# Hybrid mixer layer: two more pairs of input tiles in seven products, retention's output written over its queries, and the right operands started after the first retention

## The chip, the cores and the metric

The kernel runs on one core of one Trainium2 chip. The metric is device microseconds of one execution; a comparison uses the median of several runs. A profile is one execution recorded by the hardware profiler.

## The reference

One decoder layer over 1024 positions of width 1024, in float32. Cut to what matters here:

```python
u = rms_norm(x, norm1_g)
z = u @ w_in                                    # 3584 columns, 28 tiles of 128
cb, cc, ch = split(z[..., :1536], 3)            # conv group, 512 channels
rq, rk, rv, rg = split(z[..., 1536:], 4)        # retention group, 4 heads of 128
y_conv = group_rms_norm(cb * causal_dwconv3(cc * ch, conv_w), conv_norm_g, 8)
q, k = rotary(rq), rotary(rk) * 128 ** -0.5
o = chunkwise_retention(q, k, rv)               # chunks of 128, decay per head
y_ret = group_rms_norm(o, ret_norm_g, 4) * silu(rg)
x = x + concat([y_conv, y_ret]) @ w_out
x = x + relu(rms_norm(x, norm2_g) @ w_up) ** 2 @ w_down
out = rms_norm(x, final_norm_g)
```

Retention works chunk by chunk: `(q k^T * decay) v` inside a chunk, plus `q` times a state carried from chunk to chunk.

## The kernel before

Activations lie transposed: features on the 128 partitions, positions along the row, so a tile `u` has 128 features and 1024 positions in two halves of 512. Each float32 factor is split into a high and a low part of a faster matmul type (`uh`, `ul` for the activations, `wh`, `wl` for a weight piece of 512 input features by 128 outputs), and a product takes three matmuls, high by high, low by high, high by low. ACT casts a raw weight piece `r` to `wh`, and DVE or POOL subtracts to get `wl` (`split_piece`). Four pieces are prepared ahead; each of the pools behind `r`, `wh` and `wl` has four buffers.

The mixer goes through these stages on PE:

- The values `v` (line 343), then eight tiles for queries and keys of two head pairs (`rot_tiles`, four tiles for each pair).
- `retention(p, q, k)` for a pair of heads, a generator in ten steps (eight chunks and two to drain). A step puts small 128x128 matmuls on PE: scores and transposed keys of chunk c, output and new state of chunk c-1, transposed output of chunk c-2. It also puts work on DVE and ACT. The first one runs while the second pair's queries and keys are multiplied, the second while the next tiles are.
- The eight tiles 0 to 7 of `IN_WHOLE`, one after the other, each by `tile_in` in 48 matmuls of 128x512 (four quarters of 12). Tiles 3i, 3i+1, 3i+2 are the three columns of conv group i. Their evacuation (`whole`, `use`) reads the PSUM bank at once.
- The four pairs of tiles of `IN_PAIRS`, each by `pair_in`: a Strassen scheme (two by two blocks in seven products instead of eight) of 7 x 12 matmuls. The left operands are sums of weight blocks, built on POOL (`Left`), and split on the fly. The right operands are the blocks `11`, `21`, `22` of `u` and four sums `t1` to `t4`, which `rights(j)` makes from freshly loaded `x` rows (`xs`) for j = 0 to 3: two DMAs, two scalings on ACT, four subtractions and three splits on DVE or POOL. `t1` is written over the second halves of `uh[0..3]`, `ul[0..3]` when the whole tiles are done. After each product DVE adds the bank to the partial sums `z`.
- When all mixer work is done, the output projection begins (operands `yh`, `yl`). Its PSUM pools take the place of the mixer's, so its first matmul waits for the last read of a mixer bank.

The order on each engine is written by a planner at build time. Engines are objects with a modelled clock; `now[0]` is the modelled PE time. After each slot of PE work (`slot`, `SLOT`), `tick` runs `background`, which lets the waiting tasks (retention, rights, conv, gate, norm) issue instructions: a task that yields `None` runs once its `ready` time lies `PE_MARGIN` back, one that yields a number once it lies that number back, one that yields engines when one of them is free within `look`, one that yields a key when `mark` has set it. `force(key)` runs everything until the key is set. Each engine then executes its queue strictly in the order written. All input DMAs are on SP's queue.

Columns of the last pair go in the order `IN_LAST = (1, 2, 6, 7, 4, 5, 3)`, which keeps two partial sums by ACT copies of the running sum `acc`.

Of the kernel before, what the change touches and what calls it, by code (L numbers as in the profile page):

```python
# [23 lines left out]
NC_ = T // P  # L24
# [10 lines left out]

IN_WHOLE = [[0, 1, 2], [3, 4, 5, 6, 7]]
IN_PAIRS = [(8, 9), (10, 11), (20, 21), (22, 23)]
IN_FIRST = [12, 13, 16, 17, 14, 15, 18, 19] + IN_WHOLE[0] + IN_WHOLE[1]  # L40
SLOT, LOOK, PE_MARGIN, LATE = 2.72, 2.0, 1.2, 0.0
NORM_MARGIN = 4.0
UP_ORDER, MLP_ORDER = (1, 2, 5, 6, 3, 7, 4), (1, 2, 6, 5, 3, 7, 4)
IN_LAST = (1, 2, 6, 7, 4, 5, 3)

# [33 lines left out]
def hybrid_layer(  # L79
# [16 lines left out]
    now, clock, procs, got = [0.0], {}, [], {}  # L96
# [23 lines left out]
    def unit(dt=F32, s="u"):  # L120
        return big.tile([P, T], dt, tag="u", name=nm(s))
# [439 lines left out]
    def retention(p, q, k):  # L561

        h0 = 2 * p
        S = pend = turn = None
        o = [unit(s="o") for _ in range(2)]
        js = [slice(j * P, (j + 1) * P) for j in range(2)]
        if p:
            yield "retention", 0
        for c in range(NC_ + 2):
            yield None  # L570
            now[0] += 2.0
            new = None
            if c < NC_:
                sl = slice(c * P, (c + 1) * P)
                bs = bank(pr)
                for j in range(2):
                    nc.tensor.matmul(bs[:, js[j]], k[j][:, sl], q[j][:, sl], start=True, stop=True)  # L577
                kz = None
                if c < NC_ - 1:
                    bt = bs[:, 2 * P :]  # L580
                    for j in range(2):
                        nc.tensor.transpose(bt[:, js[j]], k[j][:, sl], ident)
                sc = xp.tile([P, 2 * P], F32, tag="h", name=nm("h"), bufs=6)
                for j in range(2):
                    dve.scalar_tensor_tensor(
                        sc[:, js[j]], bs[:, js[j]], by_key[:, h0 + j, c : c + 1], causal,
                        ALU.mult, ALU.mult,
                    )
                if c < NC_ - 1:
                    kz = xp.tile([P, 2 * P], F32, tag="h", name=nm("h"), bufs=6)  # L590
                    for j in range(2):
                        act.activation(
                            kz[:, js[j]], bt[:, js[j]], AF.Copy, scale=by_state[:, h0 + j, c : c + 1]
                        )
                new = (c, sc, kz)
            done, pend = pend, new
            turned, turn = turn, None
            if done is not None:
                pc, sc, kz = done
                psl = slice(pc * P, (pc + 1) * P)  # L600
                vt = v[pc // 2]
                v0 = (pc % 2) * H + h0 * P
                vj = [vt[:, v0 + j * P : v0 + (j + 1) * P] for j in range(2)]
                bo = bank(pr)
                for j in range(2):
                    nc.tensor.matmul(bo[:, js[j]], sc[:, js[j]], vj[j], start=True, stop=(S is None))  # L606
                    if S is not None:
                        nc.tensor.matmul(  # L608
                            bo[:, js[j]], q[j][:, psl], S[:, js[j]], start=False, stop=True
                        )  # L610
                if kz is not None:
                    bk = bo[:, 2 * P :]
                    for j in range(2):
                        nc.tensor.matmul(bk[:, js[j]], kz[:, js[j]], vj[j], start=True, stop=True)  # L614
                    Sn = xp.tile([P, 2 * P], F32, tag="S", name=nm("S"), bufs=2)
                    if S is None:
                        dve.tensor_copy(Sn, bk)
                    else:
                        for j in range(2):
                            dve.scalar_tensor_tensor(  # L620
                                Sn[:, js[j]], S[:, js[j]], gammas[h0 + j] ** P, bk[:, js[j]],
                                ALU.mult, ALU.add,
                            )
                    S = Sn

                on = xp.tile([P, 2 * P], F32, tag="h", name=nm("h"), bufs=6)
                m = xp.tile([P, 2], F32, tag="m", name=nm("m"), bufs=4)
                for j in range(2):
                    act.activation(
                        on[:, js[j]], bo[:, js[j]], AF.Square, accum_out=m[:, j : j + 1]  # L630
                    )
                dve.scalar_tensor_tensor(
                    m, m, 1.0 / P, by_query[:, h0 : h0 + 2, pc], ALU.mult, ALU.add
                )
                m = rsqrt(m, xp.tile([P, 2, 2], F32, tag="m2", name=nm("m"), bufs=4))
                for j in range(2):
                    act.activation(on[:, js[j]], bo[:, js[j]], AF.Copy, scale=m[:, j : j + 1])
                turn = (pc, on)
            if turned is not None:
                pc, on = turned  # L640
                b = bank(pr)
                for j in range(2):
                    nc.tensor.transpose(b[:, js[j]], on[:, js[j]], ident)
                for j in range(2):
                    act.copy(o[j][:, pc * P : (pc + 1) * P], b[:, js[j]])
                    if pc % 4 == 3:
                        o_n[h0 + j, pc // 4] = o[j]
                        mark(("o", h0 + j, pc // 4), act)
            retention_task[p].ready = max(clock[act], clock[dve])
            if c == NC_:  # L650
                mark(("retention", p), act)

# [111 lines left out]

    def rights(j):

        if j:
            yield "retention", 1
        a, b = xs[j], xs[4 + j] = [unit(s="xs") for _ in range(2)]
        lo_, hi_ = hs  # L770
        for k, t in ((j, a), (4 + j, b)):
# [42 lines left out]
    def pair_in(fs, last):  # L814
# [3 lines left out]
        for at, n in enumerate(order):  # L818
# [9 lines left out]
            if n == 2:  # L828
                dve.tensor_add(c11, acc, b)
                ready = 0, 0  # L830
            if n in (6, 7, 4):
                dve.tensor_add(acc, acc, b)
            if n == 4:
                ready = 1, 0
            if last:

                if n == 6:
                    act.copy(c12, acc)
                if n == 7:
                    act.copy(c22, acc)  # L840
                if n == 5:
                    dve.tensor_add(c22, c22, b)
                    dve.tensor_add(c12, c12, b)
                    ready = 1, 1
            else:
                if n == 5:
                    b5 = b
                if n == 6:
                    dve.tensor_add(c12, acc, b5)
                if n == 7:  # L850
                    dve.tensor_add(c22, acc, b5)
                    ready = 1, 1
# [477 lines left out]
    last = None  # L1330
# [147 lines left out]
```

## Time and profile before

| | |
|---|---|
| three runs | 1091.83, 1095.05, 1096.20 us; median 1095.05 |
| profiled execution | 1093.19 us, of which the span shown is 1091.4 us |
| busy over the span | PE 97%, DVE 80%, POOL 51%, ACT 43% |
| values and first 8 tiles | up to about 158 us |
| whole tiles 0 to 7 | about 158 to 266 us |
| four pairs | 266.4 to 350.9 us on PE |
| first matmul of the output projection | 362.75 us |

The rest of the span, from 362.75 us on, is the output projection and the MLP, which the change does not touch. In the views, PE, DVE, ACT, POOL and SP are the engines; a row of the time line has start, duration, engine, line, operation, output<-input, count, and in square brackets the idle time before it and what ended it. Nearly all DVE, ACT and POOL work is issued by one helper on line 73, so it is told apart by the tile names.

### The profile page before, as it was taken

What the parts mean: (1) busy time and instruction counts of PE and PEld (TensorE: products, weight loads), DVE (VectorE), ACT (ScalarE), POOL (GpSimd) and SP (SyncE); (2) the same over time, 40 slices, a digit from 0 to 9 for tenths busy, and PEclk for the clock granted to TensorE, in tenths of its full rate; (3) what the DMA queues carried; (4) which work ended last, traced back from release to release, by engine and by line L of the source; (5) the groups of instructions that cost most, each with busy time, mean ns of one, the idle gap of its engine ahead of it and who ended that gap; (6) DMA issues with size and microseconds to landing.
All of it is one profiled execution on the core that took longest, in us unless ns stands there. A gap on an engine that the chain in (4) does not pass through costs nothing.

```text
span 1091.4 us, 13980 instructions
## 1 busy us (share of the span) xinstructions
PE 1056.6 (97%) x4916; PEld 882.4 (81%) x4916; DVE 870.2 (80%) x1239; ACT 468.3 (43%) x920; POOL 558.1 (51%) x385
## 2 busy tenths in 40 slices
PE   7999999999898799989999999999999999999996
PEld 6888888887786588878888888888888888888886
DVE  7436655569988756599999989989899899899945
ACT  8211346556345444444333443443344344334453
POOL 5234343227667313448639448267276285384543
PEclk9999999999999899999999999999999999999998
DMA  7121121140111535050121211211201301210204
GB/s 271 61 59 38 40 78 40 29 155 11 58 58 45 197 97 183 1 174 20 49 87 30 69 58 40 79 37 52 91 24 49 97 20 49 88 29 11 78 1 155
DMA packets 38870, 76.50 MB, mean 70 GB/s; under 512 B 4368, under 2 KB 6544, under 8 KB 38800
## 3 DMA queue, kind: packets, MB, share of 16 engines
q1 hardware_dynamic: 38800, 75.61, 21.5%
q8 instruction: 39, 0.64, 0.3%
q14 instruction: 31, 0.25, 0.1%
HBM read 68.78 MB, written 6.82 MB: 69 GB/s over the span
## 4 chain that ended last, share of the span: by engine, by line
PE 84%; DVE 7%; issue 4%; ACT 2%; POOL 2%; DMA 1%; SPq 0%; DVEq 0%; POOLq 0%; ACTq 0%
PE b L387 56%; PE b L1228 22%; PE b L343 2%; DVE wl L73 2%; DVE x L73 1%; DVE z L73 1%; ACT wh L73 1%; PE b L606 1%; PE b L577 1%; DVE t L73 1%; POOL r L73 1%; PE b L608 1%; PE b L614 1%; PE b L324 1%; DMA wv<-w_v 1%
## 5 line engine op out<-in xcount | busy, mean ns | idle before, releaser
L73 ACT CAST wh<-r 128x512 fp32r<-128x512 f32 x286 | 177.0, 621 | 347.4 <-PE b L387 169.7
L73 DVE TENSOR_TENSOR wl<-r,wh 128x512 fp32r<-128x512 f32 x256 | 238.1, 932 | 95.7 <-ACT wh L73 93.7
L387 PE MATMUL b<-U,wh 128*128 128x512 f32 x992 | 306.0, 389 | 3.3 <-DVE U L73 3.0
L73 POOL TENSOR_TENSOR r<-r,r 128x512 f32<-128x512 f32 x136 | 210.2, 1548 | 122.4 <-DVE wl L73 70.7
L1228 PE MATMUL b<-V,wh 128*128 128x512 f32 x784 | 241.9, 389 | 0.4 <-POOL V L73 0.4
L387 PEld LDWEIGHTS b<-U,wh 128*128 128x128 f32 x992 | 186.0, 188 | 42.7 <-DVE U L73 3.4
L73 DVE TENSOR_TENSOR x<-x,b 128x512 f32<-128x512 f32 (+1 forms) x320 | 197.9, 664 | 25.0 <-PE b L387 22.1
L387 PE MATMUL b<-U,wl 128*128 128x512 f32 x496 | 193.0, 389 | 0.0
L1228 PEld LDWEIGHTS b<-V,wh 128*128 128x128 f32 x784 | 147.2, 188 | 31.8 <-POOL V L73 0.8
L73 POOL TENSOR_TENSOR t<-t,t 128x512 f32<-128x512 f32 x70 | 105.5, 1511 | 99.2 <-ACT t L73 53.2
L1228 PE MATMUL b<-V,wl 128*128 128x512 f32 x392 | 152.5, 389 | 0.0
L73 POOL TENSOR_TENSOR wl<-r,wh 128x512 fp32r<-128x512 f32 x30 | 40.8, 1360 | 148.2 <-ACT wh L73 142.1
L387 PE MATMUL b<-ul,wh 128*128 128x512 f32 x320 | 104.9, 393 | 4.5 <-DVE ul L73 4.5
L387 PEld LDWEIGHTS b<-U,wl 128*128 128x128 f32 x496 | 93.1, 188 | 19.4
L387 PE MATMUL b<-uh,wh 128*128 128x512 f32 x320 | 106.3, 397 | 0.0
L387 PE MATMUL b<-uh,wl 128*128 128x512 f32 x320 | 104.3, 391 | 0.0
L1228 PEld LDWEIGHTS b<-V,wl 128*128 128x128 f32 x392 | 73.6, 188 | 15.1
L73 POOL TENSOR_TENSOR V<-t,V 128x512 fp32r<-128x512 f32 x35 | 49.1, 1402 | 67.2 <-ACT V L73 67.2
L73 DVE TENSOR_TENSOR t<-t,b 128x512 f32<-128x512 f32 x112 | 75.8, 677 | 1.7 <-POOL t L73 1.2
L387 PEld LDWEIGHTS b<-ul,wh 128*128 128x128 f32 x320 | 60.4, 189 | 17.8 <-DVE ul L73 4.9
L73 ACT ACTIVATE t<-t 128x512 f32<-128x512 f32 x64 | 40.2, 631 | 76.8 <-DVE t L73 76.1
L387 PEld LDWEIGHTS b<-uh,wl 128*128 128x128 f32 x320 | 60.5, 189 | 13.0
(164 smaller groups left out, 1456.4 us busy)
## 6 DMA issues: line engine op xcount, KB each, us to landing
r<-w_up_t SPq DMA_DIRECT2D x64, 256.0 KB, 2.6
r<-w_down_t SPq DMA_DIRECT2D x56, 256.0 KB, 2.6
r<-w_in_t SPq DMA_DIRECT2D x48, 256.0 KB, 2.6
xt<-xT SPq DMA_DIRECT2D x16, 256.0 KB, 5.4
xs<-xT SPq DMA_DIRECT2D x8, 512.0 KB, 5.4
r<-w_out_t SPq DMA_DIRECT2D x16, 256.0 KB, 2.6
x<-xT SPq DMA_DIRECT2D x8, 512.0 KB, 7.3
outT<-out SPq DMA_DIRECT2D x6, 512.0 KB, 2.9
```

The source lines that it names most:

```text
L73: return f(out, *args, **kw)
L324: nc.tensor.matmul(b[:, c * P : (c + 1) * P], d, ident, start=True, stop=True)
L343: nc.tensor.matmul(vb[i], a[k][:, tsl], b[k // 2][:, vs], start=(k == 0 and a is uh and b is vh), stop=(k == KT - 1 and a is ul),)
L387: nc.tensor.matmul(b, a[:, k, :], rhs(n, k)[r], start=(start and i == 0), stop=(stop and i == len(ops) - 1),)
L577: nc.tensor.matmul(bs[:, js[j]], k[j][:, sl], q[j][:, sl], start=True, stop=True)
L606: nc.tensor.matmul(bo[:, js[j]], sc[:, js[j]], vj[j], start=True, stop=(S is None))
L608: nc.tensor.matmul(bo[:, js[j]], q[j][:, psl], S[:, js[j]], start=False, stop=True)
L614: nc.tensor.matmul(bk[:, js[j]], kz[:, js[j]], vj[j], start=True, stop=True)
L1228: nc.tensor.matmul(b, a, r, start=(i == 0), stop=(i == len(ops) - 1))
```

## The change

Tiles 4 to 7 leave the whole tiles and become the pairs (4,5) and (6,7), ahead of the four pairs there were. The retention writes its output chunk into the query tile it has just used (`o = q`) instead of two new tiles. `rights(0)` and `rights(1)` start after the first retention (1 when 0 is done), 2 and 3 after the second, where 1 to 3 waited for the second before. A retention step may follow 0.3 instead of 1.2 behind its `ready` time, which is now the DVE time of its scores or state, not the later of ACT and DVE at its end; the planner looks 3.2 instead of 2.0 ahead. In the last pair two DVE additions take the place of two ACT copies.

```diff
-IN_WHOLE = [[0, 1, 2], [3, 4, 5, 6, 7]]
-IN_PAIRS = [(8, 9), (10, 11), (20, 21), (22, 23)]
+IN_WHOLE = [[0, 1, 2], [3]]
+IN_PAIRS = [(4, 5), (6, 7), (8, 9), (10, 11), (20, 21), (22, 23)]
...
-SLOT, LOOK, PE_MARGIN, LATE = 2.72, 2.0, 1.2, 0.0
-NORM_MARGIN = 4.0
+SLOT, LOOK, PE_MARGIN, LATE = 2.72, 3.2, 1.2, 0.0
+NORM_MARGIN, STEP_MARGIN = 4.0, 0.3
...
-        o = [unit(s="o") for _ in range(2)]
+        o = q
...
-            yield None
-            now[0] += 2.0
+            yield STEP_MARGIN
+            now[0] += 1.7
...
                 new = (c, sc, kz)
+                retention_task[p].ready = clock[dve]
...
                     S = Sn
+                    retention_task[p].ready = clock[dve]
...
-            retention_task[p].ready = max(clock[act], clock[dve])
+            if c >= NC_ - 1:
+                retention_task[p].ready = clock[act]
...
-        if j:
-            yield "retention", 1
+        yield "retention", j // 2
+        if j == 1:
+            yield "t4", 0
...
+            if last and n in (6, 7):
+                dve.tensor_add(c12 if n == 6 else c22, acc, b)
             if n in (6, 7, 4):
                 dve.tensor_add(acc, acc, b)
...
-                if n == 6:
-                    act.copy(c12, acc)
-                if n == 7:
-                    act.copy(c22, acc)
```

In all, 24 matmuls of 128x512 go (four tiles of 48 become two pairs of 84). DVE gets 26 instructions more, ACT 4 and POOL 4; SP issues as many DMAs as before.

The first place is DVE's queue where the second retention ends and the late right operands begin. `m` are the retention's small norm factors, `xs` and `U` the right operands, `z<-b,R` the evacuation of a whole tile. Before, this stands behind tile 4 (`a_1940` and `cv_2124` are conv group 1):

```order
L73 TENSOR_TENSOR m_2098<-m_2098 128x2
L73 SCALAR_TENSOR_TENSOR m_2098<-m_2098,m_2094 128x2
L73 SCALAR_TENSOR_TENSOR m_2098<-m_2098 128x2
L73 TENSOR_TENSOR a_1940<-a_1940,ssq 128x512
L73 SCALAR_TENSOR_TENSOR cv_2124<-a_1940,sm,cv_2124 128x511
L73 SCALAR_TENSOR_TENSOR cv_2124<-a_1940,sm,cv_2124 128x510
L73 SCALAR_TENSOR_TENSOR cv_2124<-a_1940,sm,cv_2124 128x512 x2
L73 TENSOR_TENSOR xs_2110<-xs_2110 128x512
L73 TENSOR_TENSOR xs_2110<-xs_2111,xs_2110 128x512
```

Now it stands around the evacuation of tile 2 (`z_1968`):

```order
L73 TENSOR_TENSOR m_1926<-m_1926 128x2
L73 SCALAR_TENSOR_TENSOR m_1926<-m_1926,m_1922 128x2
L73 SCALAR_TENSOR_TENSOR m_1926<-m_1926 128x2
L73 TENSOR_TENSOR U_1946<-xs_1613,U_1946 128x512
L73 TENSOR_TENSOR z_1968<-b_1790,R 128x512
L73 TENSOR_TENSOR z_1968<-b_1791,R 128x512
L73 TENSOR_TENSOR z_1968<-z_1968,cv_1786 128x512 x2
L73 TENSOR_TENSOR xs_1938<-xs_1938 128x512
L73 TENSOR_TENSOR xs_1938<-xs_1939,xs_1938 128x512
```

The last step of the second retention has moved from behind tile 4 to the end of tile 2, the right operands of j = 0 and 1 (`U_1946` is the last of them) are done by then, and those of j = 2 (`xs_1938`) follow tile 2. From this first `xs` row to the last addition of the last pair DVE's queue held 119 instructions before and holds 152 now.

The second place is ACT's queue in the last pair. `wh` are the casts of weight pieces, `yh` those of finished outputs. Before:

```order
L73 CAST wh_3008<-r_2771 128x512
L73 COPY z_2939<-z_2940 128x512
L73 ACTIVATE z_2939<-z_2939 128x512
L73 CAST yh_3019<-z_2588 128x512
L73 CAST wh_3038<-r_2894 128x512
L73 COPY z_2940<-z_2940 128x512
L73 CAST yh_3044<-o_834 128x512
L73 CAST yh_3048<-o_835 128x512
L73 CAST wh_3068<-r_2930 128x512
```

and now:

```order
L73 ACTIVATE z_2966<-z_2966 128x512
L73 CAST wh_3040<-r_2801 128x512
L73 CAST yh_3048<-q_604 128x512
L73 CAST yh_3051<-q_605 128x512
L73 CAST wh_3070<-r_2938 128x512
L73 CAST wh_3094<-r_2959 128x512
L73 CAST yh_3099<-q_943 128x512
L73 CAST wh_3121<-r_2985 128x512
```

The two `COPY z` rows, each of which reads a sum that DVE must have written, no longer stand ahead of the weight casts.

## The prediction

> **What bounds the kernel now.** First the page's busy line, then the waits of PE, then windows cut where PE's waits are.
>
> ```profile
> PE 1056.6 (97%) x4916; PEld 882.4 (81%) x4916; DVE 870.2 (80%) x1239; ACT 468.3 (43%) x920; POOL 558.1 (51%) x385
> ...
> PE b L387 <- DVE z L73: 11.8, 1, 11.8
> PE b L387 <- DVE ul L73: 4.5, 1, 4.5
> PE b L387 <- DVE U L73: 3.0, 1, 3.0
> ```
>
> PE is busy for 97%, so over the whole span it is the bound, and a matmul saved counts where PE does not wait. Its two longest waits are both in the stretch that the change rewrites: 4.5 us for `ul` (the `t1` operands at the start of the pairs) and 11.8 us for DVE's last read of a mixer bank, ahead of the output projection. The third is later.
>
> ```profile
> core 0: us, PE busy (x) PEld busy (x) DVE busy (x) ACT busy (x) POOL busy (x), PEclk, DMA share, GB/s
> 158.00:200.00 42.00, 42.00 (x231) 36.06 (x231) 24.66 (x55) 20.48 (x69) 15.80 (x12) 1.00 0.14 38
> 200.00:240.80 40.80, 40.80 (x226) 35.26 (x225) 20.80 (x53) 23.45 (x73) 12.18 (x9) 1.00 0.31 110
> ...
> 350.90:362.70 11.80, 0.07 (x1) 0.00 (x0) 9.94 (x13) 5.14 (x10) 5.46 (x6) 0.71 0.20 67
> 240.80:362.70 121.90, 105.70 (x458) 86.60 (x456) 111.61 (x121) 64.09 (x104) 83.77 (x55) 0.96 0.15 46
> 362.70:372.80 10.10, 10.05 (x37) 8.22 (x38) 9.13 (x11) 5.41 (x10) 4.90 (x3) 0.83 0.96 356
> ```
>
> Until 240.8 us DVE is busy for about half the time (45.5 of 82.8 us) and PE never waits. From 240.8 to 362.7 us, where the right operands and the pairs are, DVE is busy for 111.6 of 121.9 us. So in this stretch DVE, not PE, says when the mixer ends. The rows of PE and DVE there:
>
> ```profile
> 266.41 0.39 PE L387 MATMUL b<-uh,wh 128*128 128x512 f32 x1
> 271.85 0.39 PE L387 MATMUL b<-uh,wh 128*128 128x512 f32 x1
> 276.71 0.50 PE L387 MATMUL b<-ul,wh 128*128 128x512 f32 x1 [4.46 <-DVE ul L73]
> 350.58 0.39 PE L387 MATMUL b<-uh,wl 128*128 128x512 f32 x1
> 362.75 0.77 PE L387 MATMUL b<-yh,wh 128*128 128x512 f32 x1 [11.78 <-DVE z L73]
> ...
> 240.81 0.68 DVE L73 TENSOR_TENSOR xs<-xs 128x512 f32<-128x512 f32 x1
> 361.93 0.67 DVE L73 TENSOR_TENSOR z<-z,b 128x512 f32<-128x512 f32 x1
> ```
>
> The pairs start on PE at 266.41, the third product waits at 271.85, PE is through at 350.9 and then waits for the last `z<-z,b` of DVE, which ends at 362.60. What moves the end of the mixer is therefore what moves that last addition. The sum is made to 362.75 us; what follows is the same code in the same order.
>
> **The change, part by part.**
>
> *PE.* Matmuls follow each other at 0.227 us, and a normalization in between costs 2 x 0.23:
>
> ```profile
> 238.44 19.07 PE b L387 x84
> 257.51 0.23 PE b L467
> 257.74 0.23 PE b L468
> 257.96 2.72 PE b L387 x12
> ```
>
> 24 matmuls fewer are 24 x 0.227 = 5.4 us. When does PE reach the pairs? Four tiles fewer stand ahead of them (4 x 48 x 0.227 = 43.6 us), as do four normalizations (1.8 us), which come later now; retention's matmuls are as many as before, and all of them still come ahead. 266.4 - 43.6 - 1.8 = 221.0 us. From there 42 products of 2.72 us and 8 normalizations are 114.2 + 3.7 = 117.9: PE could be through at 338.9, 12 us before its old 350.9. The 5.4 us are in this.
>
> *DVE, price of one instruction.* The same kind of instruction takes two times here:
>
> ```profile
> 257.94 1.78 DVE L73 TENSOR_TENSOR U<-xs,U 128x512 fp32r<-128x512 f32 x1
> 259.64 0.68 DVE L73 TENSOR_TENSOR xs<-xs,xs 128x512 f32<-128x512 f32 x1
> 260.25 0.68 DVE L73 TENSOR_TENSOR wl<-r,wh 128x512 fp32r<-128x512 f32 x1
> ...
> 184.97 1.28 POOL L73 TENSOR_TENSOR wl<-r,wh 128x512 fp32r<-128x512 f32 x1 [6.05 <-ACT wh L73]
> 255.73 3.44 POOL L73 TENSOR_TENSOR r<-r,r 128x512 f32<-128x512 f32 x2
> 261.06 1.62 POOL L73 TENSOR_TENSOR r<-r,r 128x512 f32<-128x512 f32 x1 [1.89 <-issue]
> ...
> L73 DVE TENSOR_TENSOR z<-z,b 128x512 f32<-128x512 f32 x28 | 18.9, 679 | 0.4 <-PE b L387 0.2
> ```
>
> While POOL rests (259.2 to 261.1) one follows the other at 0.61 us (259.64, 260.25); while POOL works it takes 1.78, 1.1 us more. Additions from a bank stay at 0.68 on average. Of the 111.6 busy us from 240.8 on, 121 x 0.61 = 73.8 are the work, and 37.8 us are spent beside POOL, 0.69 for each of its 55 instructions (34 slow ones among DVE's 83 that read no bank, 41%). An instruction of POOL by itself takes 1.28.
>
> *DVE, the new queue.* From the first late `xs` row to the last addition it holds 152 instructions where there were 119: 16 additions from banks more, 6 subtractions of weight pieces more on each of DVE and POOL, the conv work of tiles 4 to 7 without a bank as source, against one set of right operands fewer, since j = 1 is done earlier. POOL has 63 instructions beside them. 152 x 0.61 = 92.7 and 63 x 0.69 = 43.5 make 136.2 us; by shares, 41% of the 100 that read no bank at 1.1 us are 45 and the sum 137.8. I take 137.
>
> *DVE, its idle time.* Before, 121.9 - 111.6 = 10.3 us. In the last pair this is where it came from:
>
> ```profile
> 348.97 0.62 ACT L73 COPY z<-z 128x512 f32<-128x512 f32 x1 [5.86 <-DVE z L73]
> 351.18 1.79 DVE L73 TENSOR_TENSOR wl<-r,wh 128x512 fp32r<-128x512 f32 x1 [1.14 <-ACT wh L73]
> 353.60 0.62 ACT L73 COPY z<-z 128x512 f32<-128x512 f32 x1 [2.45 <-DVE z L73]
> 355.81 0.82 DVE L73 TENSOR_TENSOR wl<-r,wh 128x512 fp32r<-128x512 f32 x1 [1.58 <-ACT wh L73]
> 306.53 0.78 DVE L73 TENSOR_TENSOR wl<-r,wh 128x512 fp32r<-128x512 f32 x1 [1.09 <-PE b L468]
> ```
>
> ACT's two copies wait for DVE's sums, the weight casts queue behind the copies, and DVE waits for these: 2.7 us. The change takes the copies out and gives DVE two additions (1.2 us, in the 152), so this pays about 1.5 us net. The 1.09 at 306.53 arose where DVE had caught up with PE and was no delay of its own. 6.5 us are left, and over a stretch longer by an eighth 7.5.
>
> *When DVE starts there.* The late `xs` rows stand behind the evacuation of tile 2, which PE ends one tile (10.9 us) ahead of the pairs, at 210.1. Two reads of banks and two further products, 4 instructions, take 2.4 to 4.8 us: 213.5. DVE must have no backlog then. What comes earlier is retention:
>
> ```profile
> 185.70 0.60 DVE L73 SCALAR_TENSOR_TENSOR h<-b,bk,causal 128x128 f32<-128x128 f32 x2
> 186.73 0.49 DVE L73 SCALAR_TENSOR_TENSOR S<-S,b 128x128 f32<-128x128 f32 x2 [0.42 <-PE b L614]
> 187.97 0.16 DVE L73 SCALAR_TENSOR_TENSOR m<-m,bq 128x2 f32<-128x2 f32 x1 [0.75 <-ACT h L73]
> ```
>
> A step is 0.60 + 0.49 + 4 x 0.16 = 1.7 us of DVE, five steps 8.7. `rights(0)` and `rights(1)` put 11 instructions on DVE there, 6.7 to 20 us, about 11, and some 5 us of that kind were there before. So about 15 us more go into 158 to 210 us, where DVE had 17.3 + 5 = 22 us idle by the windows. That idle time is the cover at which I cost them nothing; if half of it falls where nothing is ready, 4 us come on top.
>
> The last addition then ends at 213.5 + 137 + 7.5 = 358.0 against 362.6: **-4.6 us**. PE's 338.9 is hidden behind that, and its waits only change place: the first `ul` row is DVE's 13th from 213.5, about 213.5 + 13 x 0.9 = 225 to 230, against PE's 221.0 + 2 x 2.72 + 0.9 = 227.4, so the 4.5 us shrink to 0 to 3, and PE then waits some 15 us for DVE towards the end. The bounds: with no DVE instruction slowed the end is PE's, 339 to 345; at the old 1.02 us for every instruction, idle time included (121.9 / 119), it is 213.5 + 155.7 = 369.
>
> *The rest.* Output over the queries: the same 32 copies into other tiles, nothing; four large buffers come free, and the late `xs` loads need not wait for most of theirs. SP issues as many DMAs; the `xs` loads stand behind weight pieces in its queue, and weight pieces behind them, but four pieces are always ahead (10.9 us of PE work). I cost it at nothing; without that cover a landing is a few us.
>
> **The rivals.**
>
> *DVE keeps up and PE sets the end (faster).* If POOL's instructions fall beside bank reads (52 of the 152, where it was 38 of 121), the blocked time drops to 0.45 for each, 28 us, and with 4 us idle DVE is done at 338; then the end is PE's, with a tail of 5 to 9 us: 346. PE's last wait is below 9 us, and part of the 1.7 us lost to the slow clock behind the old one (10.1 us at 0.83) comes back. 1093.2 - 16.8 = 1076.5. Against it: 41% slow is what nearly this mix gave.
>
> *POOL blocks DVE for more (slower).* One mechanism, in the pairs: DVE's instructions with two SBUF sources meet POOL more often, because POOL's queue is longer too. Each more costs 1.1 us. With 41 slow the end is at 358; 50 of 100 give 368, the point from which the kernel is slower by more than 0.5%, and 55 give 374: 1104.8. For it: the change adds DVE work just where DVE was already the bound.
>
> The Trainium skill's page "SBUF — State Buffer", section "SBUF: two separate sides", states that VectorE and GpSimd take a shared port pair by an exclusive lock for a whole instruction, the loser blocking fully, and only VectorE instructions with two SBUF inputs (or in a two-port mode) are concerned. By that rule taken to its end every one of POOL's 63 would hold DVE for a full instruction, 1.28 us, and the end would be at 394, 1124 in all; the trace agrees with who is blocked, but half of POOL's instructions meet a DVE that waits or reads a bank, so I go by 0.69 and count that end within this rival's chance.
>
> *Dense retention steps stall PE (about the same).* A step now follows after 12 matmuls (2.7 us) where there were 24.
>
> ```profile
> 184.53 0.60 PE L577 MATMUL b<-q,q 128*128 128x128 f32 x4
> 186.53 0.38 PE L643 MATMUL b<-ident,h 128*128 128x128 f32 x2
> 188.99 0.62 ACT L73 ACTIVATE h<-b,m 128x128 f32<-128x128 f32 x2 [0.62 <-DVE m L73]
> ```
>
> The chain from the step's output through ACT and DVE ends at 189.6; the next step's transposes, which need it, would come at 186.7 + 2.7 + 2.0 = 191.4. 1.8 us of slack, less than one slowed DVE instruction and an ACT cast ahead. If half of 16 steps lose 1 us, all starts 8 us later: 366, or 1096.5.
>
> **How the numbers follow.** The profiled execution (1093.19) is 1.9 us below the median of 1095.05, within the runs' spread of 4.4, so I add 1 us for a median. The likeliest case (0.50) is -4.6: 1089.5, with its own range 1084 to 1094. PE sets the end: 0.25, 1077.5. POOL blocks more: 0.12, 1106. Retention stalls: 0.13, 1097.5. A change of 0.5% (5.5 us) is about what a measurement of this kernel can tell. Against 1095 a time below 1089.5 is faster by that: half of the likeliest case less a little (0.21) and all of the second, 0.46. Slower: 0.12 and a little of the fourth, 0.14. The same: 0.40. The range 1076 to 1101 leaves out about 0.1 at each end.
>
> **What would show it.** In the profile after: 24 matmuls fewer; DVE busy for over 90% from about 213 to 358 us, with 152 instructions in about 137 busy us; the first pair's first matmul near 221; PE through near 340 to 350 and a wait of about 10 us for DVE's `z` ahead of the first `yh` matmul near 358; no ACT copy in the last pair. I am wrong if PE waits in retention's steps, if DVE has idle time in the pairs (then PE or ACT leads), or if DVE's mean there is not near 0.9 us.

## The result and the profile after

The changed kernel takes 1098.49 us (median of 12 runs, 1096.21 to 1099.35), the kernel before 1094.17 us (12 runs, 1091.83 to 1096.20). The ratio is 1.0037, 95% interval 1.0027 to 1.0047: slower by 4 us where 4.6 less at the mixer's end were forecast. The profiled execution took 1099.35 us, its span is 1097.6 us.

The lines of the page and of PE's waits (after the colon: us in all, times, longest):

```profile
PE 1057.9 (96%) x4892; PEld 878.5 (80%) x4892; DVE 893.7 (81%) x1265; ACT 468.9 (43%) x924; POOL 565.3 (52%) x389
```

```profile
PE b L387 <- DVE z L73: 9.3, 1, 9.3
PE b L387 <- DVE ul L73: 4.0, 1, 4.0
PE b L387 <- DVE wl L73: 3.5, 3, 2.0
...
PE b L645 <- ACT h L73: 1.9, 4, 0.8
```

PE has its 24 matmuls fewer. It waits in more places: for `ul` as before, now for weight pieces (`wl`) too, and in retention's transposes (L645), where it did not wait before. The windows, in the columns shown with the prediction:

```profile
158.00:200.00 42.00, 41.59 (x251) 36.61 (x249) 27.26 (x59) 22.93 (x71) 16.00 (x12) 1.00 0.28 92
200.00:218.20 18.20, 17.29 (x90) 14.33 (x91) 13.69 (x35) 13.92 (x46) 4.75 (x4) 1.00 0.23 93
218.20:366.30 148.10, 129.53 (x548) 103.01 (x546) 142.06 (x153) 70.83 (x119) 101.11 (x66) 0.95 0.16 49
366.30:377.00 10.70, 10.55 (x35) 8.49 (x36) 7.39 (x10) 4.78 (x9) 4.16 (x3) 0.73 0.93 349
```

DVE works for 142.1 of the 148.1 us from the first late `xs` row to the mixer's end, for 153 instructions. Its rows at both ends of that stretch, and PE's:

```profile
214.65 1.28 DVE L73 TENSOR_TENSOR z<-b,R 128x512 f32<-128x512 f32 x2
215.85 2.39 DVE L73 TENSOR_TENSOR z<-z,cv 128x512 f32<-128x512 f32 x2
218.16 1.78 DVE L73 TENSOR_TENSOR xs<-xs 128x512 f32<-128x512 f32 x1
...
365.63 0.67 DVE L73 TENSOR_TENSOR z<-z,b 128x512 f32<-128x512 f32 x1
```

```profile
224.30 0.39 PE L387 MATMUL b<-uh,wh 128*128 128x512 f32 x1
236.08 0.79 PE L387 MATMUL b<-ul,wh 128*128 128x512 f32 x1 [3.98 <-DVE ul L73]
353.68 0.50 PE L387 MATMUL b<-uh,wl 128*128 128x512 f32 x1 [2.01 <-DVE wl L73]
356.57 0.63 PE L387 MATMUL b<-uh,wl 128*128 128x512 f32 x1
366.45 0.76 PE L387 MATMUL b<-yh,wh 128*128 128x512 f32 x1 [9.26 <-DVE z L73]
```

The pairs start on PE at 224.30 instead of 266.41, and yet the first `yh` matmul is at 366.45 instead of 362.75: 3.7 us later, which is nearly all of the 4.3 between the medians. (In the two profiled executions the rest of the program differs by another 2.5 us, with a granted clock of 0.73 for 10 us after the wait where it was 0.83. Over all kernels of this document this rest lies between 728.2 and 731.2 us, in the same code and in no order that I could find; I take the mixer's end as the measure, and beside it the ratio.)

### The profile page after: what moved, and what is told of

It reads as the page before. It is cut to its first block, busy times and chain, and to the rows that moved or that the text cites. A ratio compares the mean times of both kernels' runs of the same rounds, so it can differ in the third digit from the quotient of the medians.

```text
span 1097.6 us, 13986 instructions
## 1 busy us (share of the span) xinstructions
PE 1057.9 (96%) x4892; PEld 878.5 (80%) x4892; DVE 893.7 (81%) x1265; ACT 468.9 (43%) x924; POOL 565.3 (52%) x389
## 4 chain that ended last, share of the span: by engine, by line
PE 80%; DVE 10%; issue 3%; DMA 2%; ACT 2%; POOL 2%; SPq 0%; POOLq 0%; DVEq 0%; ACTq 0%
PE b L387 52%; PE b L1230 23%; PE b L343 2%; DVE wl L73 2%; DVE q L73 1%; DMA wv<-w_v 1%; POOL r L73 1%; DVE xs L73 1%; DVE z L73 1%; DVE U L73 1%; DVE t L73 1%; DMA r<-w_in_t 1%; DVE m L73 1%; ACT h L73 1%; DVE x L73 1%
## 5 line engine op out<-in xcount | busy, mean ns | idle before, releaser
L387 PE MATMUL b<-U,wh 128*128 128x512 f32 x1040 | 321.9, 391 | 3.6 <-DVE U L73 3.0
L73 POOL TENSOR_TENSOR r<-r,r 128x512 f32<-128x512 f32 x144 | 222.4, 1547 | 125.4 <-DVE wl L73 72.8
L387 PEld LDWEIGHTS b<-U,wh 128*128 128x128 f32 x1040 | 195.7, 188 | 45.1 <-DVE U L73 3.4
L387 PE MATMUL b<-U,wl 128*128 128x512 f32 x520 | 203.2, 391 | 0.2 <-DVE wl L73 0.2
L73 POOL TENSOR_TENSOR wl<-r,wh 128x512 fp32r<-128x512 f32 x36 | 51.4, 1432 | 143.9 <-ACT wh L73 143.3
L387 PE MATMUL b<-ul,wh 128*128 128x512 f32 x288 | 98.0, 394 | 4.0 <-DVE ul L73 4.0
L387 PE MATMUL b<-uh,wl 128*128 128x512 f32 x288 | 97.8, 394 | 3.3 <-DVE wl L73 3.3
L387 PE MATMUL b<-uh,wh 128*128 128x512 f32 x288 | 99.4, 399 | 0.0
L73 DVE TENSOR_TENSOR V<-t,V 128x512 fp32r<-128x512 f32 x63 | 68.1, 1081 | 0.0
L387 PEld LDWEIGHTS b<-uh,wl 128*128 128x128 f32 x288 | 54.6, 190 | 16.2 <-DVE wl L73 4.5
```

The costliest lines, as they stand in the source:

```text
L73: return f(out, *args, **kw)
L387: nc.tensor.matmul(b, a[:, k, :], rhs(n, k)[r], start=(start and i == 0), stop=(stop and i == len(ops) - 1),)
```

## The experiments

Two theories stood at the start. One: the two added pairs give DVE more time than they take from PE, and POOL's instructions, which block DVE, are a large part of it. The rival: the pairs gain, and the parts moved with them (retention's dense steps, the early right operands) lose. All ratios are to the kernel before. "End" is the start of the first `yh` matmul. In some kernels line 387 has become 389, 394 or 395.

### Which part costs: four pairs, six pairs alone, the copies alone

```diff
-IN_WHOLE = [[0, 1, 2], [3]]
-IN_PAIRS = [(4, 5), (6, 7), (8, 9), (10, 11), (20, 21), (22, 23)]
+IN_WHOLE = [[0, 1, 2], [3, 4, 5, 6, 7]]
+IN_PAIRS = [(8, 9), (10, 11), (20, 21), (22, 23)]
```

> The change with four pairs again (tiles 4 to 7 whole); retention's pace, the output over the queries, the right operands after the first retention and the missing ACT copies stay. Theory (the six pairs are what costs): DVE's queue from the first late `xs` row holds 119 instructions as before, less the 10 of the right operands for j = 1, plus 2 for the copies, 111; at the 0.94 busy us that one took before (111.6 / 119) they are busy 104 us, with 10.3 - 2.7 = 7.6 us idle. If the queue starts at 240.8 + 2 us, as late as retention's waits have made the pairs, the first `yh` matmul is near 355, 8 us before that of the kernel before, and the kernel takes 1086, ratio 0.993. Rival (retention's pace and the early right operands are what costs): they lose the same 3 to 5 us here, the end does not come before 362, and the ratio is 1.000 to 1.005, the same as with all of the change.

Measured: 0.9994 (0.9984 to 1.0003), end 362.0. In its number this is nearer the rival's end of 362 and ratio of 1.000, but the rival wanted the same as with all of the change, and that is 1.0037: the rest of the change does neither good nor harm to the time, and what lost 4 us are the two pairs, given that rest. My 355 was wrong all the same. The windows of this kernel and, under them, of the kernel before, cut at 274.9 us, where the `ul` rows of DVE begin in both:

```profile
274.90:310.00 35.10, 34.82 (x154) 28.47 (x153) 33.62 (x37) 15.16 (x27) 24.78 (x17) 1.00 0.17 53
310.00:362.00 52.00, 39.54 (x170) 30.98 (x169) 49.02 (x56) 27.42 (x44) 34.91 (x23) 0.94 0.19 56
218.20:362.00 143.80, 131.06 (x572) 106.40 (x571) 119.69 (x137) 67.72 (x113) 80.28 (x54) 0.98 0.15 46
```

```profile
274.90:310.00 35.10, 33.29 (x140) 27.35 (x141) 30.93 (x38) 14.88 (x24) 24.19 (x16) 0.95 0.18 53
310.00:362.70 52.70, 40.97 (x181) 33.52 (x179) 46.88 (x53) 27.74 (x45) 34.79 (x25) 0.93 0.18 56
```

In the four pairs DVE has as many instructions as before (93, 91), has lost its idle time (4.5 us instead of 10.0), and is busy for 4.8 us more. The two additions are 1.4 of these; the rest is the same kind of work taking longer. And four pairs against six, from 218.2 us on: the two added pairs give DVE 142.1 - 119.7 = 22.4 busy us, against 24.1 - 6.0 = 18.1 us that it had idle, nearly all while PE worked on whole tiles (18.9 of the 24.1 lie between 240.8 and 274.9 us). The difference, 4.3 us, is how much later the end is (366.3 against 362.0). That the two agree is arithmetic, since a stretch is busy and idle time; what the traces give is the size of each. That is where the 24 matmuls went.

The six pairs alone, in the kernel before, are the same edit the other way round:

> The kernel before with the six pairs alone; retention keeps its pace of one step to 24 matmuls. Theory (the pairs cost DVE more than they save PE): DVE gets the 16 bank additions and the further weight subtractions, POOL its own; from about 213 us on DVE has 152 + 10 (right operands of j = 1, now late again) - 2 = 160 instructions, at 0.93 us 149 busy and 10 idle: the end is near 372, 10 us after that of before, ratio 1.008 to 1.01. Rival (the pairs gain and the other parts spoil it): 24 matmuls fewer on PE show as 5.4 us, ratio 0.995.

Measured: 1.0172 (1.0155 to 1.0189), end 380.4.

```profile
PE b L387 <- DVE z L73: 15.5, 2, 12.4
PE b L387 <- ACT uh L73: 12.0, 1, 12.0
...
PE b L643 <- ACT h L73: 4.0, 3, 1.9
```

The sign was the theory's, the size was not (1.008 to 1.010 and 372 were expected): PE stops for 12.0 us where the pairs begin, since the right operands come behind retention. The parts that go with the pairs don't spoil them: they win back some 15 us of this.

The last pair's two additions on DVE in place of ACT's copies, in the kernel before:

```diff
+            if last and n in (6, 7):
+                dve.tensor_add(c12 if n == 6 else c22, acc, b)
...
-                if n == 6:
-                    act.copy(c12, acc)
-                if n == 7:
-                    act.copy(c22, acc)
```

> The kernel before with one part of the change: in the last pair two additions on DVE write the two sums that ACT copied. Theory (the prediction's step): the 1.14 and 1.58 us that DVE waited for ACT's `wh` casts behind the copies go, 1.2 us of additions come: 1.5 us net, the first `yh` matmul near 361, ratio 0.9985. Rival: the additions stand beside POOL and the waits only move to another operand: no change, ratio 1.000.

Measured: 0.9999 (0.9990 to 1.0008), end 361.2. DVE's wait for `wh`, before and with the edit:

```profile
DVE wl L73 <- ACT wh L73: 7.0, 8, 1.6
```

```profile
DVE wl L73 <- ACT wh L73: 4.7, 7, 1.2
```

The end is 1.5 us earlier, as the prediction had it, but no gain in the time could be measured (0.9985 was expected, outside the interval).

### What DVE's time is made of: sums and additions left out

```diff
+            def psum(f, o, a, b):
+                if mixing:
+                    clock[pool] = max(clock[pool], now[0]) + pool.cost(H)
+                else:
+                    f(o, a, b)
...
-                pool.tensor_sub(a11, a21, a11)
+                psum(pool.tensor_sub, a11, a21, a11)
```

> The change, with POOL's 24 weight sums in the six pairs left out (the products then take weight blocks that are not summed); the planner counts them as if they were there, so that the order of the other work stays. Theory (POOL's instructions block DVE's, 0.69 us each, and DVE's queue sets the mixer's end): of 142 busy us on DVE from 218 to 366 us 24 x 0.69 = 16.6 go; the end comes as much earlier until PE sets it, PE having worked for all but about 20 us of the stretch: the first `yh` matmul between 348 and 352, ratio about 0.985 to 0.988. Rival (DVE is slow there for its own operands' sake, or PE and ACT set the end): DVE's mean stays at 0.93 us, the end within 3 us of 366, ratio 1.001 to 1.004.

Measured: 0.9888 (0.9873 to 0.9903), end 350.3.

```profile
218.20:350.30 132.10, 123.97 (x548) 102.37 (x547) 124.81 (x152) 70.79 (x119) 65.97 (x43) 0.99 0.18 54
```

DVE has the same work (152 instructions) and 17.25 us less busy time: 0.72 us for each instruction that POOL no longer executes. The end is 16.1 us earlier. DVE sets the mixer's end after the change, and POOL makes about a third of its busy time (66 x 0.72 = 47.5 of 142.1); the rival is out.

Then additions of DVE's own:

```diff
-            if n in (6, 7, 4):
+            if n in (6, 7):
+                clock[dve] = max(clock[dve], now[0]) + dve.cost(H, "", True)
+            if n == 4:
                 dve.tensor_add(acc, acc, b)
```

> The change, with 12 of DVE's additions from banks left out (`acc += b` after the products 6 and 7 of six pairs, so part of the sums is missing); the planner counts them as if they were there. Theory (DVE's queue sets the mixer's end): they took 0.68 us each after the change, 12 x 0.68 = 8.2, and the first `yh` matmul comes at 366.4 - 8.2 = 358, ratio 0.996. Rival (PE or ACT leads and DVE only follows): DVE gets 8 us of idle time more, the end stays at 366, ratio 1.004.

Measured: 1.0008 (0.9997 to 1.0019), end 365.0: between the theory's 0.996 and 358 and the rival's 1.004 and 366, nearer the rival in the end. The window and the group of weight subtractions here, and under them groups of the change (busy us, mean ns, idle time before):

```profile
218.20:365.00 146.80, 128.98 (x548) 103.71 (x547) 140.04 (x141) 70.96 (x119) 101.39 (x66) 0.95 0.17 49
```

```profile
L73 DVE TENSOR_TENSOR wl<-r,wh 128x512 fp32r<-128x512 f32 x25 | 29.5, 1181 | 2.3 <-ACT wh L73 1.8
```

```profile
L73 DVE TENSOR_TENSOR z<-z,b 128x512 f32<-128x512 f32 x44 | 29.8, 679 | 0.7
L73 DVE TENSOR_TENSOR wl<-r,wh 128x512 fp32r<-128x512 f32 x25 | 28.2, 1130 | 1.4 <-ACT wh L73 1.1
L73 DVE SCALAR_TENSOR_TENSOR z<-r,z 128x512 f32<-128x512 f32 x8 | 10.4, 1300 | 0.3
```

Twelve instructions and 8.2 us of work are gone, and DVE is busy for only 2 us less. The additions read a bank and are not blocked (0.679 us, with POOL at work for two thirds of the time); while they ran, POOL's instructions went by at no cost. Without them more of these meet an instruction with two SBUF operands: besides `wl`, the eight `z<-z,less_g,r` went from 1.118 to 1.332 us. So these additions were nearly free beside POOL. (The time moved further than the end: 1.0008 against 1.0037 is some 3 us, of which the end's 1.4 explains half.) That POOL costs a fixed 0.7 us for each of its instructions, as I had it until then, is wrong.

The weight sums moved to DVE:

```diff
+            eng = dve if mixing else pool
...
-                pool.tensor_sub(a11, a21, a11)
+                eng.tensor_sub(a11, a21, a11)
```

> The change, with POOL's 24 weight sums in the six pairs done by DVE. Theory (each instruction of POOL costs DVE 0.72 us by blocking it, as leaving the sums out showed: 17.25 us for 24): DVE wins 17.3 and gets 24 x 0.61 = 14.6, so the end is 2 to 3 us earlier, near 364, ratio 1.001. Rival (DVE was slow for other reasons, and POOL takes work off it): DVE gets 14.6 us and wins nothing, the end is near 381, ratio 1.017.

Measured: 1.0076 (1.0061 to 1.0091), end 370.7, between the two and later than without the edit.

```profile
218.20:370.60 152.40, 132.84 (x547) 104.89 (x545) 143.27 (x164) 70.80 (x119) 84.89 (x56) 0.93 0.15 47
```

The planner gave POOL 14 other instructions in their place, so that only 10 changed sides (56 on POOL, 164 on DVE). For DVE's 11 more and POOL's 10 fewer the theory has 11 x 0.61 - 10 x 0.72 = 0.5 us less busy time, the rival 6.7 more; measured are 1.2 more. So this is nearer the theory, and work moved from POOL to DVE was about even for DVE's busy time here. The rest of the 4 us is idle time of DVE, 9.1 us instead of 6.0. The two forecasts of the end, 364 and 381, were made for 24 instructions and decide nothing.

### Retention's pace

```diff
-SLOT, LOOK, PE_MARGIN, LATE = 2.72, 3.2, 1.2, 0.0
+SLOT, LOOK, PE_MARGIN, LATE = 2.72, 2.0, 1.2, 0.0
...
-            yield STEP_MARGIN
-            now[0] += 1.7
+            yield None
+            now[0] += 2.0
...
-            if c >= NC_ - 1:
-                retention_task[p].ready = clock[act]
+            retention_task[p].ready = max(clock[act], clock[dve])
```

> The change, with retention at its old pace (one step to 24 matmuls, the planner's look of 2.0, the old times at which a step may follow); six pairs, early right operands, output over the queries and the last pair's additions stay. In PE's order the last four steps then stand with 6 matmuls or none between them, as in the six pairs alone. Theory (the pace is what the six pairs need, and the dense steps' 1.9 us of waits are its price): PE waits over 10 us for retention and the right operands behind it, the first `yh` matmul is near 380, ratio 1.014 to 1.018, as with the six pairs alone (1.017). Rival (the early right operands are what they need): the 1.9 us of waits go, the pairs begin near 222, the end is near 364, ratio 1.001.

Measured: 1.0077 (1.0063 to 1.0092), end 371.0.

```profile
PE b L387 <- ACT uh L73: 7.3, 1, 7.3
...
PE b L643 <- ACT h L73: 3.8, 3, 1.8
```

PE waits where the theory had it, but the end moved by 4.5 us instead of some 13. So with six pairs the dense steps, with the planner's longer look, gain 4.4 us (1.0077 against 1.0037), and the other 10 that lie between this and the six pairs alone are the early right operands' and the two small parts' (I did not take these apart).

### Relieving DVE: a second operand in a bank

If only instructions with two SBUF operands are blocked, a subtraction whose second operand lies in a bank is safe. ACT has time:

```diff
-        act.copy(hi, raw)
...
-        eng.tensor_sub(lo, raw, f32(hi))
+        sub = f32(hi)
+        if paired and eng is dve:
+            b = pr.tile([P, 4, P], F32R, tag="b", name=nm("b"))
+            act.copy(b, raw)
+            sub = f32(b)
+        act.copy(hi, raw)
+        eng.tensor_sub(lo, raw, sub)
```

> The change, and in the six pairs ACT writes the high part of a weight piece a second time, into a PSUM bank, and DVE's subtraction `wl` takes it from there: the same result, one 0.62 us cast more on ACT for each, and DVE reads one operand from SBUF instead of two. Theory (POOL blocks only DVE's instructions with two SBUF operands): the 25 `wl` go from 1.13 to 0.68 us, 11 us, and the rest stays: end near 355, ratio 0.993 to 0.995. Rival 1 (each instruction of POOL blocks something for 0.72 us whatever is there): the blocked time moves to the next instruction with two SBUF operands, the end stays at 366, ratio 1.004. Rival 2 (ACT's 15 us more, 0.6 us ahead of each `wl`, become the wait): DVE's idle time for `wh` grows by 5 us and more, end 360 or later.

Measured: 0.9970 (0.9959 to 0.9982), end 358.5: the theory's sign, 8 of its 11 us. The first rival, with its end at 366, is out.

```profile
218.20:358.20 140.00, 126.15 (x544) 102.67 (x542) 133.94 (x155) 84.05 (x142) 93.15 (x62) 0.96 0.17 50
```

```profile
L73 DVE TENSOR_TENSOR wl<-r,b 128x512 fp32r<-128x512 f32 x22 | 14.9, 678 | 0.7 <-ACT b L73 0.6
L73 DVE SCALAR_TENSOR_TENSOR z<-r,z 128x512 f32<-128x512 f32 x8 | 11.4, 1424 | 0.3
```

Those 22 `wl` that read a bank take 0.678 us instead of 1.130, with POOL at work for 67% of the stretch instead of 68%. A part moves on: `z<-r,z` went from 1.300 to 1.424. DVE is busy for 8.1 us less, with two instructions more. ACT's casts delay nothing that shows: DVE is idle for 6.1 us, as it was (6.0).

With this the runs gave a rule. For each window take 0.68 us for an instruction of DVE that reads a bank and 0.61 for each other; what is left of its busy time is blocked time:

```
                        DVE instr.  reading   busy   POOL     share of work   blocked us
                        in all      a bank    us     instr.   without a bank  per POOL instr.
sums left out           152         52        124.8  43       0.63            0.66
after the change        153         52        142.1  66       0.64            0.68
sums on DVE             164         53        143.3  56       0.65            0.71
additions left out      141         40        140.0  66       0.69            0.78
cast in a bank          155         74        133.9  62       0.50            0.55
and less in its bank    157         82        129.0  63       0.45            0.44
and rt in a bank        158         92        125.7  62       0.39            0.37

kernel before           121         38        111.6  55       0.66            0.64
four pairs              137         44        119.7  54       0.65            0.61
six pairs alone         154         54        131.3  66       0.62            0.51
retention's old pace    153         56        127.8  71       0.61            0.43
four pairs, cast        141         59        113.8  51       0.55            0.46
four, less and rt too   142         76        110.8  50       0.44            0.38
```

For the change: 52 x 0.68 + 101 x 0.61 = 97.0, share 61.6 / 97.0, blocked 45.1 / 66. In the upper seven rows an instruction of POOL costs DVE 0.94 to 1.12 us times the share of work without a bank. The first five made the rule, at 1.08; the next two came after it. The lower six rows, counted in the same way, give less, 0.71 to 0.96: there DVE idles for 8 to 19% of the stretch, in the upper ones for 4 to 7%. That POOL can't block a DVE that is idle would explain it, but no run tests that alone. So the rule is rough, and one for a DVE that hardly ever waits. The Trainium skill's page "SBUF — State Buffer", section "SBUF: two separate sides", says that only VectorE instructions with two SBUF inputs, or in a two-port mode, share a lock with GpSimd. These runs agree on who is blocked (0.678 against 1.130). By its lock, the later of the two waits until the earlier one has ended; the 1.1 us at a meeting are nearly a whole POOL instruction of 1.28.

> The change with four pairs again, and the cast into a bank as in the run before with six. The runs so far give a working rule: DVE's blocked time (busy time less 0.68 us for each instruction that reads a bank and 0.61 for each other) for each instruction of POOL is 1.08 us times the share of DVE's work that reads no bank: 0.68 after the change (share 0.64), 0.78 with the 12 additions left out (0.69), 0.55 with the cast in a bank (0.50). Theory (this rule; DVE leads in the pairs whatever their number): in the four pairs alone DVE had 82.6 busy us in 87; 16 `wl` into banks take the share from 0.61 to 0.44 and 5 us off: first `yh` matmul near 357, ratio 0.994, no better and no worse than six pairs with the cast (0.997). Rival (with the cast DVE is no longer the bound, so the six pairs' 24 matmuls fewer count): four pairs end 5 us later than six, near 363, ratio 1.001.

Measured: 0.9941 (0.9929 to 0.9952), end 356.3. The ratio and the end are the theory's; DVE is busy for 5.9 us less than in the four pairs without the cast, where 5 were expected.

```profile
218.20:356.30 138.10, 129.89 (x572) 106.89 (x571) 113.83 (x141) 78.05 (x130) 73.40 (x51) 0.98 0.16 48
```

The same edit gains more with four pairs than with six, and four are now ahead by 0.3% (0.9941 against 0.9970), where the expectation had them level. The account is that of before: the two added pairs are 133.9 - 113.8 = 20.1 busy us for DVE against 18.2 us of idle time (24.3, 6.1), 1.9 us too much.

Then two steps that add no instruction. First the norms' `less` goes back to the bank that it came from, and the products take all their banks from one pool:

```diff
-        dve.scalar_tensor_tensor(less, b, EPS / inv_n, less, ALU.add, ALU.mult)
-        yield from done(rt, less)
+        dve.scalar_tensor_tensor(b, b, EPS / inv_n, less, ALU.add, ALU.mult)
+        yield from done(rt, b)
...
-            b = product(n, (pm, pr)[at % 2])
+            b = product(n, pm)
```

> The change with the cast into a bank, and two edits that add no instruction: the norms' `less` is written back to the bank that it was read from, so that 8 of the late `z` instructions on DVE read one operand from SBUF instead of two; the products take their banks from one pool, since the other now holds these. Theory (the rule, blocked time for each instruction of POOL 1.08 us times the share without a bank): 82 of 155 read banks, base 100.3 us, share 0.44, 62 x 0.48 = 30 blocked, 130 busy where it was 134: first `yh` matmul near 354.5, ratio 0.9935. Rival (banks held longer make ACT, DVE or PE wait for one): end 358 or later, ratio 0.997 or more.

Measured: 0.9922 (0.9910 to 0.9934), end 353.9.

```profile
218.20:353.90 135.70, 125.75 (x550) 102.34 (x548) 129.03 (x157) 85.32 (x143) 93.29 (x63) 0.99 0.17 53
```

DVE is busy for 129.0 us, the rule's 130 within 1 us. (The pool of the products was not changed by itself.) Then `rt`:

```diff
-        rt = xp.tile([P, H], F32, tag="s", name=nm("r"), bufs=4)
+        rt = bank(pr)
```

> As the kernel with `less` in its bank, and `rt` in a bank of its own too, so that 16 of the late `z` instructions read one operand from SBUF. Theory (the rule): 90 of 155 read banks, base 100.9, share 0.39, 62 x 0.42 = 26 blocked, 127 busy: end near 351.5, ratio 0.991, where PE's own waits begin to set it. Rival (two banks for each norm, two norms under way, four banks: the casts queue behind the norms): DVE and PE wait for casts, end 356 or later, ratio 0.995 or more.

Measured: 0.9906 (0.9891 to 0.9921), 1085.69 us, end 353.5.

```profile
218.20:353.50 135.30, 125.74 (x549) 102.18 (x547) 125.72 (x158) 85.66 (x145) 89.35 (x62) 0.98 0.17 53
```

```profile
PE b L394 <- DVE z L73: 7.9, 3, 6.9
```

DVE's busy time is the rule's (126 against 127), the end is not (353.5 against 351.5): DVE is idle for 9.6 us, and PE is as busy as DVE, 125.7 of 135.3 us. Which of the two sets the end now isn't shown. This is the lowest time of all that compute the whole, below both kernels; what `rt` adds to `less` is within the noise (0.9906 against 0.9922).

> The last kernel (casts, `less` and `rt` in banks) with four pairs instead of six. With six it took 0.9906 of the kernel before; the first `yh` matmul came at 353.5, PE having waited for 7.9 us in the pairs where it had waited for 20 after the change. Theory (the six pairs lost because DVE's share of a pair took longer than PE's; with DVE relieved PE leads and its 24 matmuls fewer count): four pairs end 3 to 5 us later, near 357, ratio 0.993 to 0.995, where with only the cast in a bank six were 3 us behind four (0.997 against 0.994). Rival (a pair costs on DVE what it saves on PE whatever DVE's load): four are as far ahead as before or level, end 350 to 353, ratio 0.988 to 0.9905.

Measured: 0.9927 (0.9911 to 0.9943), end 355.2.

```profile
218.20:355.20 137.00, 129.98 (x572) 106.97 (x572) 110.75 (x142) 78.07 (x131) 71.93 (x50) 0.99 0.15 49
```

The two added pairs now give DVE 125.7 - 110.8 = 15.0 busy us against 16.6 of idle time (26.2, 9.6): 1.7 us to the good at the mixer's end. Six pairs come out ahead, as the theory has it, by less than it said, and the intervals of the two ratios overlap; that six are faster in the time itself is not shown. What is shown is that the two pairs' loss at the end shrinks with the busy time that they give DVE: 4.3 us later, 1.9 later, 1.7 earlier, for 22.4, 20.1 and 15.0 us.

## Why the prediction was wrong

**The bound was right.** DVE's queue sets the mixer's end, and POOL takes a third of its time; the runs with sums left out and with operands in banks show both. PE has 24 matmuls fewer, and ends its pairs with a wait for `z` (9.3 us, about 10 were foreseen), though at 357 us instead of 340 to 350.

**Two terms of the sum were too small**, DVE's start and its busy time, and together they turned its sign: 213.5 + 137 + 7.5 = 358.0 was forecast, 218.2 + 142.1 + 6.0 = 366.3 came.

- *When DVE starts (213.5, measured 218.2).* PE reached the pairs at 224.30, not 221.0. I had costed PE's way through the dense steps at nothing and given their stalls to a rival. They came: 1.9 us of waits for ACT's `h`, in four places; the rest of the 3.3 us I can't name. The longest is this one, with the rows of DVE and POOL that stand ahead of it:

```profile
196.30 0.91 DVE L73 TENSOR_TENSOR m<-m 128x2 f32<-128x2 f32 x1 [0.27 <-ACT m L73]
197.25 1.21 DVE L73 SCALAR_TENSOR_TENSOR m<-m,m 128x2 f32<-128x2 f32 x1
198.49 1.19 DVE L73 SCALAR_TENSOR_TENSOR m<-m 128x2 f32<-128x2 f32 x1
...
195.90 1.29 POOL L73 TENSOR_TENSOR xs<-xs 128x512 f32<-128x512 f32 x1
197.15 2.51 POOL L73 TENSOR_TENSOR a<-a,ssq 128x512 f32<-128x512 f32 x2
...
200.39 0.44 PE L645 MATMUL b<-ident,h 128*128 128x128 f32 x2 [0.80 <-ACT h L73]
```

  Three operations of 2 elements, 0.16 us each when alone, take 3.3 us beside POOL: the slack of 1.8 us that I had worked out was less than that. A further 1.4 us is `z<-z,cv` beside POOL (2.39 for two) and the evacuation ahead of it.
- *DVE's busy time (137, measured 142.1).* Counted as in the sum, with 0.61 us for each instruction, it is 153 x 0.61 = 93.3 us and 48.7 beside POOL, 0.74 for each of its 66 instructions. The sum had 92.7 and 63 x 0.69 = 43.5, in all 136.2. The instructions that it missed, one of DVE and three of POOL, are 2.7 us, the higher price 3.2. That it took 0.61 for reads of a bank too, which take 0.68, hardly matters: counted with both, as in the table, the price is 0.64 before and 0.68 after, and the forecast would have been 136.6. So the price of before did not carry over to a kernel in which DVE idles for 4% of the stretch instead of 8%; that the idle time is the reason is not shown. As a fixed price it failed altogether when the additions were left out.
- *DVE's idle time (7.5, measured 6.0)* was a little better than forecast, and took 1.5 us off the miss.

**The step behind these.** I compared DVE's end with DVE's end before, term by term, over 120 instructions, and a gain of 4.6 us hung on terms of 137 and 213 us. The comparison that decides was not made: what the two added pairs give DVE (22.4 us) against the idle time that it has while PE works on the tiles that they replace (18.1 us).

**The rivals.** PE's end (346) was not reached in any run: with the weight sums left out the end was at 350.3, with DVE relieved by 16 us of busy time at 353.5. More blocking by POOL, the slower rival, came in part: 48.7 / 1.1 = 44 slow instructions, where the sum had 41 and the rival 50. Retention's stalls came, but for 2 of the 8 us that I gave them; that this rival's 366 and 1097.5 are next to what was measured is luck. Copies and output: the copies' 1.5 us stand at the mixer's end, and could not be measured in the time. PE's wait for `ul` stayed (4.0 us of 4.5), though I had 0 to 3: DVE began 4.7 us late, and its 13 instructions to the first `ul`, most of them beside POOL, took some 17 us where I had 12 to 16.

**Left open:** what else made PE 1.4 us late ahead of the pairs, why the price of a POOL instruction rose, and why the rest of the program differs by up to 3 us between profiled executions.

## What to carry to other kernels

Where an engine is idle beside the bound, work moved onto it is paid out of that idle time: count the added busy time against the idle time of the very stretch that is replaced, before counting what the bound saves. VectorE beside GpSimd has two prices for one instruction (0.68 and 1.78 us here), so look at where its operands lie: putting one of them into a PSUM bank, even at the cost of a second cast on ScalarE, gained 0.7% against the change, and 1.3% with the operands of the norms as well, where 24 matmuls fewer on TensorE gained nothing. And an instruction that reads a bank may be nearly free on a busy VectorE, because GpSimd's work passes behind it.

## What the hardware showed that was not expected

- Twelve additions from PSUM banks, 8.2 us of work, freed 2 us of DVE when left out.
- Three DVE operations of 128 x 2 elements took 0.91 to 1.21 us beside POOL, 0.16 alone: up to 1.05 us more, about as much as the 1.1 us of an operation of 128 x 512.
- DVE's `wl` took 0.678 us with one operand in a bank and 1.130 with both in SBUF, with POOL busy for two thirds of the time in both.
